# A decoder layer on one core: the order of the convolution's transfers on GpSimd, and the place of the rotary keys

## The chip, the core and the metric

The kernel runs on one NeuronCore of a Trainium2 chip. The core has five engines, each with its own queue, worked off in order: TensorE (PE in the profile; its weight loads are PEld), VectorE (DVE), ScalarE (ACT), GpSimd (POOL) and SyncE (SP). SyncE only issues transfers here. ScalarE and GpSimd issue a few as well; all transfers run on the core's DMA engines. An instruction waits in its engine's queue until the work it depends on has finished, and everything behind it in that queue waits too.

The metric is the device time of one execution in microseconds, the median of several runs. Before the change it is 1056.4 us over 3 runs (1056.02 to 1057.13).

## The reference

One layer over 256 tokens of width 2048, all in float32. Cut to what matters:

```python
h = _rmsnorm(x, pre_norm_g)
proj = h @ w_in       # split into q_a, c_kv, k_rope, z_mla, c_in, b_gate, c_gate, z_conv, g_mla, g_conv
q  = _rmsnorm(q_a, q_a_norm_g) @ w_q_b        # 16 heads of 128 (nope) + 64 (rope)
kv = _rmsnorm(c_kv, kv_a_norm_g) @ w_kv_b     # 16 heads of 128 (k_nope) + 128 (v)
q_rope, k_rope = _apply_rope(q_rope, cos, sin), _apply_rope(k_rope, cos, sin)
# per head: scores = q_nope . k_nope + q_rope . k_rope, causal softmax, times v
y_mla  = (attn * silu(z_mla)) @ w_o_mla
u      = c_gate * c_in
conv   = conv_w[0] * u[t-2] + conv_w[1] * u[t-1] + conv_w[2] * u[t]
y_conv = (b_gate * conv * silu(z_conv)) @ w_o_conv
merged = sigmoid(g_mla) * y_mla + sigmoid(g_conv) * y_conv
x + _rmsnorm(merged @ w_out, post_norm_g)
```

The rotary part of the keys, `k_rope`, is one vector of 64 numbers per token, shared by all heads. Rotation needs a cosine and a sine for each position and frequency.

## The kernel before

**Products in two parts.** Every weight arrives as float32 and is split into a high part (`whi`, a rounded copy made by ScalarE, L224) and a low part (`wlo`, the rest, made by VectorE, L225). Activations are split likewise. A product of two such pairs takes three matmuls. The weights form one list, `plan`, of units of 128 x 2048 floats (1 MB); `take` hands out a unit and runs ahead of it: three raw units are loaded by SyncE (`load_raw`, L144) and one is split in advance (`split_unit`). A raw buffer is loaded again when its splits are done; split buffers (5 of each part) are free again when TensorE has read them.

**The order of work.** The program is built by a scheduler that places instructions on each engine by its own cost estimates and what they depend on. An instruction wrapped in `tc.keep_in_program_order` keeps, against the others so wrapped on its engine, the order in which the program text issues it. All matmuls and transposes are wrapped (L86, L89), so TensorE's order is the text's.

**The start.** The first eight units (`u_qa`) hold the activations and the query projection side by side; `latent_products` (L423) makes `qa` from them, six matmuls for each 128 features, and then `ckv`. The first three of these units go to raw buffers, the next three (the list `early`) to memory that other tiles use later: the profile shows them as `cv_f<-xw_dram` and `at_f<-xw_dram`. GpSimd meanwhile makes the rotary tables (`tables`, L359): it loads the positions, reduces the angles, and after ScalarE's sine (L398, L399) copies the results with 32 small copies (L406) to `cos_t` and `sin_t`. Its queue also holds the inverse roots of the norms (L319): `r_ckv` stands behind these copies.

**The rotary keys.** The product `kr` gives the unrotated keys in `kr_f`, which is a part of `at_f`. `key_rope` (L490) scales them (`rows`, L350) and rotates them: `rp_a` is the tile times the cosine (L416), four pieces `rp_b` the swapped quarters times the sine (L419), their sum goes back to `at_f` (L420), and `split_act` makes the two parts of `kr`, the high one on ScalarE and the low one on VectorE. First to read `kr` are the scores of head 0 (`sc<-kr,qr`). `key_rope` is called in `turn_keys`, between the two halves of the first convolution product of head 0, right after the sign is put on `sin_t` (L409).

**The first group.** Heads go in groups of two. `group_a(0)` makes `qn` and `kn` for both heads, `group_b(0)` makes `qr` (with its own rope, L524) and `vv`. Their results leave PSUM through four banks tagged `mm`, in turn: qn0, qn1, kn0, kn1, then qr takes the bank of qn0, and the two vv those of qn1 and kn0. A bank is free when VectorE has added its two halves (`whole`, L347, the tile `f`).

**The heads.** For each of 16 heads the text runs the gate product z, the scores, four quarters of a convolution product (`channels`, tile `cv`), and in between transposes, values and the next group's products. In head 0 the scores come after `channels(0, 2)`.

**The convolution.** Every fourth head completes one of four inputs for a block of 512 channels. After heads 1 and 2 of each four, `taps` (L648) is started, first for the upper 128 tokens (t = 1), then for the lower ones (t = 0). It brings the inputs shifted by one and two tokens into `mv` tiles (L654, L657; a memset L656 for the tokens before the first), and the taps, one row of 512 weights repeated over all 128 partitions, into `cw` tiles (L661, two buffers). A step later VectorE multiplies and adds (L665), and the third `cw` is loaded. All these transfers are issued by GpSimd; before the change they are not wrapped.

**The end.** `tokens` makes the merged gates and branches (tiles `sq`), then the output product (`out`), the norm and the store.

Of the kernel before, what the change touches and what calls it, by code (L numbers as in the profile page):

```python
# [18 lines left out]
P = 128  # L19
# [61 lines left out]
def tile_layer(ctx: ExitStack, tc: tile.TileContext, xw, x, pos, pvec, post_g, wc, wz, wcv, wkr, wqk, wrv, cwr, wsq, out):  # L81
    nc = tc.nc
# [111 lines left out]
    def take(i):  # L194
        ahead(i)
        parts = splits.pop(i)

        def piece(j, n):
            o = j * n
            h, o = o // HALF, o % HALF  # L200
            return parts[h][0][:, o : o + n], parts[h][1][:, o : o + n]

        return piece

    def bank(name, tag="mm", bufs=4):
        return psum.tile([P, 512], F32, name=name, tag=tag, bufs=bufs)

    def product(ps, a, b, first, last):

        (ah, al), (bh, bl) = a, b  # L210
        matmul(ps, ah, bh, start=first, stop=False)
        matmul(ps, ah, bl, start=False, stop=False)
        matmul(ps, al, bh, start=False, stop=last)
# [9 lines left out]
    def split_act(hi, lo, src, keep=False):  # L223
        a = nc.scalar.activation(hi, src, AF.Copy)  # L224
        b = nc.vector.tensor_tensor(lo, src, hi.bitcast(F32), op=ALU.subtract)  # L225
        if keep:

            tc.keep_in_program_order(a)
            tc.keep_in_program_order(b)
# [57 lines left out]
    def temp(name, shape=(P, S), dt=F32, bufs=2, tag=None):  # L287

        tag, n = tag or name.rstrip("0123456789_"), shape[-1]
        if n % LINE == 0:  # L290
            return bp.tile(list(shape), dt, name=name, tag=tag, bufs=bufs)
        return bp.tile([P, -(-n // LINE) * LINE], dt, name=name, tag=tag, bufs=bufs)[:, :n]
# [56 lines left out]
    def rows(dst):  # L349
        nc.vector.tensor_tensor(dst, dst, r_x[:, :], op=ALU.mult)  # L350

    def project(u, name, both=x_both, **kw):
        w = take(u)
        ps = bank(name, **kw)
        halves([(ps, w(k, P), both[:, k, :], k == 0, k == KD - 1) for k in range(KD)])
        return ps
# [56 lines left out]
    def rope(src, dst):  # L413

        a, b = temp("rp_a", bufs=1), temp("rp_b", bufs=1)
        nc.vector.tensor_tensor(a[:, :], src, cos_t[:, :], op=ALU.mult)  # L416
        for q in range(4):
            i, o = slice(32 * q, 32 * q + 32), slice(32 * (q ^ 1), 32 * (q ^ 1) + 32)
            nc.vector.tensor_tensor(b[o, :], src[i, :], sin_t[i, :], op=ALU.mult)  # L419
        nc.vector.tensor_tensor(dst, a[:, :], b[:, :], op=ALU.add)  # L420
# [69 lines left out]
    def key_rope():  # L490
        rows(kr_f)
        rope(kr_f, kr_f)
        split_act(kr[:, 0, :], kr[:, 1, :], kr_f)


    def pair(name, shape, bufs=1):
        return [temp(f"{name}_{n}", shape, F32R, bufs, tag=f"{name}_{n}") for n in ("hi", "lo")]
# [3 lines left out]
    def narrow(name, w, j, src):  # L501
        ps = bank(name)
        halves([(ps, w(j * KR + k, P), src[:, k, :], k == 0, k == KR - 1) for k in range(KR)])
        f = temp("f")
        whole(f[:, :], ps)
        return f
# [13 lines left out]
    def group_b(g):  # L520
        qr, vv = temp("qr", (P, HG, S), F32R, 1), pair("vv", (P, NT, HG * DV))
        w = take(u_grp[g][1])
        f = narrow(f"qr{g}", w, 0, qa)
        rope(f[:, :], f[:, :])  # L524
        for j in range(HG):

            own, other = (slice(DR * i, DR * i + DR) for i in (j, 1 - j))
            split_act(qr[own, j, :], qr[other, j, :], f[own, :])
        for t in range(NT):
            ps = bank(f"vv{g}_{t}")  # L530
            for k in range(KR):
                c = [ckv[:, k, o + t * P : o + (t + 1) * P] for o in (0, S)]
                product(ps[:, :S], c, w(2 + k, HG * DV), k == 0, k == KR - 1)
            split_act(vv[0][:, t, :], vv[1][:, t, :], ps[:, :S])
        groups[g] += [qr, vv]
# [42 lines left out]
    def turn(h, p):  # L578

        tp = bank(f"tp{h}", tag="st", bufs=1)  # L580
        for b in range(3):
            transpose(tp[:, b * P : (b + 1) * P], p[:, b * P : (b + 1) * P], ident[:, :])
        pt = temp("pt", (P, 2, 3 * P), F32R, 1)
        split_act(pt[:, 0, :], pt[:, 1, :], tp[:, : 3 * P])
        return pt
# [15 lines left out]
    def silu(name, ps):  # L601
        f, s = temp("sl_f", bufs=1), temp(name)
        whole(f[:, :], ps)
        rows(f[:, :])
        nc.scalar.activation(s[:, :], f[:, :], AF.Sigmoid)
        nc.vector.tensor_tensor(s[:, :], f[:, :], s[:, :], op=ALU.mult)
        return s
# [8 lines left out]
    cv_t = cv_f[:, :, :].rearrange("p (j t k) s -> p j t (k s)", j=4, t=NT)  # L616
    cv_ps = {}

    def channels(h, i, between=None):

        if i == 0:
            cv_ps["now"] = [bank(f"cv{h}_{t}", tag="cv", bufs=2) for t in range(NT)]
        w = take(u_head[h][1 + i])
        for t in range(NT):
            if t and between:
                between()
            for k4 in range(4):
                k = 4 * i + k4
                a = [x_both[:, k, o + t * P : o + (t + 1) * P] for o in (0, S)]
                product(cv_ps["now"][t][:, :], a, w(k4, 512), k == 0, k == KD - 1)  # L630
        if i == 3:
            channels_done(*divmod(h, 4))

    def channels_done(j, n):
        for t in range(NT):
            ps, r = cv_ps["now"][t], r_col[:, t : t + 1]
            w, u = cv_w[:, t, :], cv_t[:, j, t, :]
            if n == 0:
                nc.scalar.activation(u, ps[:, :], AF.Copy, scale=r)
            elif n == 2:  # L640
                nc.scalar.activation(w, ps[:, :], AF.Sigmoid, scale=r)
            if n:
                dst = u if n == 1 else w
                nc.vector.scalar_tensor_tensor(dst, ps[:, :], r, dst, op0=ALU.mult, op1=ALU.mult)
            if n == 3:
                nc.vector.tensor_tensor(u, u, w, op=ALU.mult)

    def taps(j, t):  # L648

        u, parts = cv_t[:, j, t, :], []  # L650
        for d in (1, 2):
            m = temp(f"mv{d}", (P, 512), bufs=1, tag=f"mv{d}x")
            if t:
                nc.gpsimd.dma_start(out=m[:d, :], in_=cv_t[P - d :, j, 0, :])  # L654
            else:
                nc.gpsimd.memset(m[:d, :], 0.0)  # L656
            nc.gpsimd.dma_start(out=m[d:, :], in_=u[: P - d, :])  # L657
            parts.append(m[:, :])
        def tap(d):
            cw = temp("cw", (P, 512), bufs=2)  # L660
            nc.gpsimd.dma_start(out=cw[:, :], in_=cwr[2 - d : 3 - d, 512 * j : 512 * (j + 1)].to_broadcast([P, 512]))  # L661
            return cw

        def join(dst, a, b, op):
            tc.keep_in_program_order(nc.vector.tensor_tensor(dst, a, b, op=op))  # L665

        cws = [tap(d) for d in (1, 2)]
        yield
        for a, cw in zip(parts, cws):
            join(a, a, cw[:, :], ALU.mult)  # L670
        join(parts[0], parts[0], parts[1], ALU.add)
        cw = tap(0)
        yield
        join(u, u, cw[:, :], ALU.mult)
        join(u, u, parts[0], ALU.add)
        yield

    cv_w = bp.tile([P, NT, 512], F32, name="cv_w")
    for h in range(H):
        sz = silu("sz", project(u_head[h][0], f"z{h}"))  # L680
        if h == 0:
            latent_turn("qa", qa, "q_g", (("st", 1), ("o", 1)))
            def turn_keys():
                latent_turn("ckv", ckv, "kv_g", (("mm", 4), ("mm", 4)))
                next(table_parts)
                key_rope()
        else:
            if h == 1:
                values(0, pt, sz0)
            p = scores(h)  # L690
        channels(h, 0, None if h else turn_keys)
        if h == 0:
            group_a(0)
            group_b(0)
        channels(h, 1)
        if h > 0:
            pt = turn(h, p)
        if h % 4 > 1:
            next(tap)
        channels(h, 2)  # L700
        if h > 0:
            values(h, pt, sz)
            if h % 4 > 1:
                next(tap)
            values_next(h)
        else:
            p = scores(h)
        channels(h, 3)
        if h % 4 in (1, 2):

            tap = taps(h // 4, 2 - h % 4)
            next(tap)
        if h == 0:
            values_next(h)
            pt, sz0 = turn(h, p), sz
# [52 lines left out]
    for c in range(4):  # L768
# [12 lines left out]
        m = gates[0]  # L781
# [170 lines left out]
```

## Time and profile before

| what | before |
|---|---|
| median of 3 runs | 1056.4 us (1056.02 to 1057.13) |
| the profiled execution | 1056.16 us, its span 1054.4 us |
| granted TensorE clock | 0.998 |
| VectorE busy | 669.8 us (64%) |
| ScalarE busy | 563.2 us (53%) |
| GpSimd busy | 70.5 us (7%) |
| bytes moved | 212.17 MB, mean 201 GB/s |

The profile is of one execution. Times in it count from the start of the span in microseconds; a row of the order of time gives start, duration, engine, line, operation, output and inputs, and in square brackets how long the engine was idle before it and what ended that. "x4" after a form means that four neighbouring instructions were merged into the row. A line can be that of a helper, so all matmuls bear L86. Matmuls overlap: the next starts before the last has ended. In a table by stretches each engine has its busy time and the number of its instructions; the last three columns are the granted clock (1.00 is full), the mean busy share of the DMA engines and the bytes per second in GB.

### The profile page before, as it was taken

What the parts mean: (1) busy time and instruction counts of PE and PEld (TensorE: products, weight loads), DVE (VectorE), ACT (ScalarE), POOL (GpSimd) and SP (SyncE); (2) the same over time, 40 slices, a digit from 0 to 9 for tenths busy, and PEclk for the clock granted to TensorE, in tenths of its full rate; (3) what the DMA queues carried; (4) which work ended last, traced back from release to release, by engine and by line L of the source; (5) the groups of instructions that cost most, each with busy time, mean ns of one, the idle gap of its engine ahead of it and who ended that gap; (6) DMA issues with size and microseconds to landing.
All of it is one profiled execution on the core that took longest, in us unless ns stands there. A gap on an engine that the chain in (4) does not pass through costs nothing.

```text
span 1054.4 us, 13093 instructions
## 1 busy us (share of the span) xinstructions
PE 1044.4 (99%) x5030; PEld 879.5 (83%) x5030; DVE 669.8 (64%) x962; ACT 563.2 (53%) x778; POOL 70.5 (7%) x147
## 2 busy tenths in 40 slices
PE   9999999999999999999999999999999999999997
PEld 7888888888888888888888888888888888888885
DVE  7587677865787767777676765554554455445562
ACT  7777556566665566645656464434444434443450
POOL 7520010000010000100001000000000000000000
PEclk9999999999999999999999999999999999999999
DMA  8755466654675545755467455555555555558552
GB/s 324 313 193 190 160 220 200 229 200 150 220 229 200 200 166 205 235 194 200 156 217 246 172 198 176 184 200 184 188 190 196 200 190 187 182 200 307 195 176 80
DMA packets 33311, 212.17 MB, mean 201 GB/s; under 512 B 4256, under 2 KB 4960, under 8 KB 10848
## 3 DMA queue, kind: packets, MB, share of 16 engines
q1 hardware_dynamic: 29232, 197.54, 53.1%
q0 software_dynamic: 3584, 10.50, 3.6%
q10 hardware_dynamic: 432, 3.29, 0.8%
q8 instruction: 39, 0.64, 0.2%
q14 instruction: 24, 0.20, 0.1%
HBM read 205.05 MB, written 2.10 MB: 196 GB/s over the span
## 4 chain that ended last, share of the span: by engine, by line
PE 93%; POOL 2%; issue 1%; DVE 1%; DMA 1%; ACT 1%; SPq 0%; POOLq 0%; DVEq 0%; ACTq 0%
PE sq L86 33%; PE cv L86 33%; PE z L86 8%; PE out L86 7%; PE vv L86 2%; PE kn L86 2%; PE qn L86 2%; PE sc L86 1%; PE qa L86 1%; PE ckv L86 1%; DMA cv_f<-xw_dram 1%; PE qr L86 1%; PE o L86 1%; POOL cos_t L406 1%; POOL sin_t L406 1%
## 5 line engine op out<-in xcount | busy, mean ns | idle before, releaser
L225 DVE TENSOR_TENSOR wlo<-raw,whi 128x1024 fp32r<-128x1024 f32 (+1 forms) x370 | 440.8, 1199 | 308.9 <-ACT whi L224 279.4
L224 ACT ACTIVATE whi<-raw 128x1024 fp32r<-128x1024 f32 (+1 forms) x372 | 384.0, 1036 | 370.3 <-PE sq L86 187.5
L86 PE MATMUL cv<-whi,x_both 128*128 128x512 f32 x1024 | 325.5, 391 | 0.0
L86 PEld LDWEIGHTS cv<-whi,x_both 128*128 128x128 f32 x1024 | 192.3, 188 | 38.7
L86 PE MATMUL cv<-wlo,x_both 128*128 128x512 f32 x512 | 199.6, 390 | 0.0
L86 PE MATMUL sq<-whi,x_both 128*128 128x512 f32 x512 | 160.2, 391 | 0.0
L86 PEld LDWEIGHTS sq<-whi,x_both 128*128 128x128 f32 x512 | 96.1, 188 | 19.8
L86 PEld LDWEIGHTS cv<-wlo,x_both 128*128 128x128 f32 x512 | 96.2, 188 | 18.5
L86 PE MATMUL sq<-wlo,x_both 128*128 128x512 f32 x256 | 99.6, 389 | 0.0
L86 PE MATMUL sq<-whi,at_both 128*128 128x512 f32 x256 | 80.4, 391 | 0.0
L86 PE MATMUL sq<-whi,cv_both 128*128 128x512 f32 x256 | 79.4, 389 | 0.0
L86 PE MATMUL out<-whi,m_both 128*128 128x512 f32 x256 | 79.3, 390 | 0.0
L86 PE MATMUL z<-x_both,whi 128*128 128x512 f32 x256 | 60.8, 390 | 0.0
L86 PEld LDWEIGHTS sq<-whi,cv_both 128*128 128x128 f32 x256 | 48.1, 188 | 10.0
L86 PEld LDWEIGHTS sq<-whi,at_both 128*128 128x128 f32 x256 | 48.1, 188 | 9.9
L86 PEld LDWEIGHTS out<-whi,m_both 128*128 128x128 f32 x256 | 48.1, 188 | 9.9
L86 PEld LDWEIGHTS sq<-wlo,x_both 128*128 128x128 f32 x256 | 48.1, 188 | 9.8
L86 PEld LDWEIGHTS z<-x_both,whi 128*128 128x128 f32 x256 | 47.9, 188 | 9.9
L86 PE MATMUL sq<-wlo,at_both 128*128 128x512 f32 x128 | 49.8, 389 | 0.0
L86 PE MATMUL sq<-wlo,cv_both 128*128 128x512 f32 x128 | 49.8, 389 | 0.0
L86 PE MATMUL out<-wlo,m_both 128*128 128x512 f32 x128 | 49.8, 389 | 0.0
L86 PEld LDWEIGHTS z<-x_both,wlo 128*128 128x128 f32 x256 | 32.8, 191 | 1.2
(209 smaller groups left out, 1068.1 us busy)
## 6 DMA issues: line engine op xcount, KB each, us to landing
raw<-wsq_dram SPq DMA_DIRECT2D x80, 1024.0 KB, 4.7
raw<-wcv_dram SPq DMA_DIRECT2D x64, 1024.0 KB, 4.8
raw<-wz_dram SPq DMA_DIRECT2D x16, 1024.0 KB, 4.7
raw<-wqk_dram SPq DMA_DIRECT2D x8, 1024.0 KB, 5.8
cw<-cwr_dram POOLq DMA_DIRECT2D x24, 256.0 KB, 4.0
raw<-wrv_dram SPq DMA_DIRECT2D x8, 768.0 KB, 4.3
raw<-wc_dram SPq DMA_DIRECT2D x4, 1024.0 KB, 10.0
cv_f<-x_dram SPq DMA_DIRECT2D x1, 2048.0 KB, 9.4
```

The source lines that it names most:

```text
L86: return tc.keep_in_program_order(nc.tensor.matmul(*a, **kw))
L224: a = nc.scalar.activation(hi, src, AF.Copy)
L225: b = nc.vector.tensor_tensor(lo, src, hi.bitcast(F32), op=ALU.subtract)
L406: tc.keep_in_program_order(nc.gpsimd.tensor_copy(dst[to, SQ * q : SQ * (q + 1)], src[ti, :]))
```

## The change

The transfers and memsets of `taps` are now wrapped in `keep_in_program_order`, through a small function `bring`. And `key_rope()` is called no more in `turn_keys` but after `group_b(0)`.

```diff
     def taps(j, t):
 
         u, parts = cv_t[:, j, t, :], []
+
+        def bring(dst, src):
+
+            tc.keep_in_program_order(nc.gpsimd.dma_start(out=dst, in_=src))
+
         for d in (1, 2):
             m = temp(f"mv{d}", (P, 512), bufs=1, tag=f"mv{d}x")
             if t:
-                nc.gpsimd.dma_start(out=m[:d, :], in_=cv_t[P - d :, j, 0, :])
+                bring(m[:d, :], cv_t[P - d :, j, 0, :])
             else:
-                nc.gpsimd.memset(m[:d, :], 0.0)
-            nc.gpsimd.dma_start(out=m[d:, :], in_=u[: P - d, :])
+                tc.keep_in_program_order(nc.gpsimd.memset(m[:d, :], 0.0))
+            bring(m[d:, :], u[: P - d, :])
             parts.append(m[:, :])
         def tap(d):
             cw = temp("cw", (P, 512), bufs=2)
-            nc.gpsimd.dma_start(out=cw[:, :], in_=cwr[2 - d : 3 - d, 512 * j : 512 * (j + 1)].to_broadcast([P, 512]))
+            bring(cw[:, :], cwr[2 - d : 3 - d, 512 * j : 512 * (j + 1)].to_broadcast([P, 512]))
             return cw
...
             def turn_keys():
                 latent_turn("ckv", ckv, "kv_g", (("mm", 4), ("mm", 4)))
                 next(table_parts)
-                key_rope()
...
         if h == 0:
             group_a(0)
             group_b(0)
+            key_rope()
         channels(h, 1)
```

In the built program, GpSimd's queue before the change has two `cw` transfers right behind the four position loads at the start, ahead of the mask and the tables; after the change they stand behind the first four `mv` transfers, at the end of head 1. The later `cw` loads, which before stood as far ahead as their buffers allowed, now follow the `mv` transfers of their own block. On VectorE the first rope product of the keys (`rp_a`) moves from behind L350 of the keys, and the four `rp_b`, the sum and the low split of `kr` from among the group's operations, to the end of the group's operations: `rp_a` and `rp_b` behind the sum of the queries' rope, the sum behind the two low splits of `qr`, the low split of `kr` one weight split later. On ScalarE the high split of `kr` moves likewise. TensorE and SyncE have the same instructions in the same order.

## The prediction

> **What bounds the kernel now.** I read the first page, then the waits of TensorE, then the order of time on each engine from 4 to 17 us and from 59 to 90 us.
>
> ```profile
> PE 1044.4 (99%) x5030; PEld 879.5 (83%) x5030; DVE 669.8 (64%) x962; ACT 563.2 (53%) x778; POOL 70.5 (7%) x147
> PE 93%; POOL 2%; issue 1%; DVE 1%; DMA 1%; ACT 1%; SPq 0%; POOLq 0%; DVEq 0%; ACTq 0%
> ```
>
> TensorE is busy for 99% of the span and makes 93% of the chain that ended last. What VectorE, ScalarE or GpSimd lose or gain therefore counts only where TensorE stands still. Its waits say where that is:
>
> ```profile
> PE qa L86 <- ACT whi L224: 0.9, 1, 0.9
> PE qr L86 <- DVE f L347: 0.2, 1, 0.2
> ```
>
> These are two single waits, and both lie where the change reaches: one in the first query products, while the early loads run, and one in the first group's products. Busy time hides part of such a loss, because a product that waits is drawn longer, so I take each loss from the spacing of starts. The first, TensorE in order of time:
>
> ```profile
> 12.43 1.13 PE L86 MATMUL qa<-whi,x_both 128*128 128x512 f32 x4
> 13.40 0.62 PE L86 MATMUL qa<-wlo,x_both 128*128 128x512 f32 x2
> 14.94 1.19 PE L86 MATMUL qa<-whi,x_both 128*128 128x512 f32 x4 [0.92 <-ACT whi L224]
> 15.97 0.62 PE L86 MATMUL qa<-wlo,x_both 128*128 128x512 f32 x2
> 16.43 1.07 PE L86 MATMUL qa<-whi,x_both 128*128 128x512 f32 x4
> 17.35 0.62 PE L86 MATMUL qa<-wlo,x_both 128*128 128x512 f32 x2
> 17.80 0.39 PE L86 MATMUL qa<-whi,x_both 128*128 128x512 f32 x1
> ```
>
> A step of six products takes 17.80 - 16.43 = 1.37. Two steps from 12.43 would end at 15.17; the next one begins at 16.43. **The early loss is 1.26 us.** The second place, with the same shapes of the next group behind it, from the chain of waits:
>
> ```profile
> 71.48 1.09 PE L86 MATMUL kn<-ckv,whi 128*128 128x512 f32 x4
> 72.42 0.63 PE L86 MATMUL kn<-ckv,wlo 128*128 128x256 f32 x4
> 73.20 1.19 PE L86 MATMUL qr<-qa,whi 128*128 128x512 f32 x4 [0.15 <-DVE f L347]
> 74.24 0.63 PE L86 MATMUL qr<-qa,wlo 128*128 128x256 f32 x4
> 75.00 0.38 PE L86 MATMUL vv<-whi,ckv 128*128 128x256 f32 x1
> 75.23 0.28 PE L86 MATMUL vv<-wlo,ckv 128*128 128x256 f32 x1
> ```
>
> ```profile
> 125.71 1.40 PE qr L86 x8
> 127.11 2.88 PE vv L86 x24
> ```
>
> Undisturbed, such a block of eight (kn has the shapes of qr) takes 1.40 and one vv product 2.88 / 24 = 0.12. So qr was due at 72.88, vv at 74.28 and its second product at 74.40; it began at 75.23. **The group's loss is 0.83 us.** Together 2.09 us: the most that removing these two waits can return.
>
> **Part 1: two cw transfers leave the start.** The tap weights `cw` depend on nothing, and before the change the scheduler put the first two at the head of GpSimd's queue; now they stand behind the four `mv` transfers at the end of head 1. At the start they run while the weights of the first products arrive. GpSimd's issue, its queue from 4 to 13 us, and the DMA share there and a little later:
>
> ```profile
> 3.99 1.10 POOL L661 DMA_DIRECT2D cw<-cwr_dram  x2
> ```
>
> ```profile
> q0 software_dynamic: 287, 0.56, 25.1%
> ```
>
> ```profile
> 4.00:13.00 9.00, 9.00 (x40) 7.45 (x39) 7.04 (x13) 5.75 (x11) 5.57 (x13) 1.00 1.02 339
> 18.00:22.00 4.00, 4.00 (x19) 3.31 (x18) 4.00 (x8) 4.00 (x10) 3.32 (x9) 1.00 1.02 427
> 69.20:87.60 18.40, 18.11 (x98) 15.43 (x97) 18.10 (x34) 11.37 (x21) 0.00 (x0) 1.00 0.52 185
> ```
>
> The DMA engines are full in 4 to 13 us (share 1.02), and GpSimd's queue has 25.1% of them: 0.56 MB, nearly all of it the two `cw` (128 x 512 floats each, 0.52 MB together). What TensorE waits for at 14.94 is ScalarE, and ScalarE waits for the fourth load:
>
> ```profile
> 13.86 0.51 ACT L299 ACTIVATE x_both<-cv_f,pv 128x256 fp32r<-128x256 f32 x1 [1.54 <-DMA cv_f<-xw_dram]
> 14.28 0.61 ACT L224 ACTIVATE whi<-cv_f 128x512 fp32r<-128x512 f32 x1
> ```
>
> Without the two transfers this load lands earlier by 0.52 MB at the 427 GB/s that the weights reach alone at 18 to 22 us, 1.23 us, or by up to 25.1% of 9 us = 2.26 us. TensorE was due at 12.43 + 1.37 = 13.80 instead of 14.94, so a landing 1.14 earlier is enough, and both prices exceed it. After that ScalarE needs 0.51 + 0.61 for a step against 1.37 on TensorE, so it is not late next. The later loads are issued as VectorE frees buffers and move along with it. Bounds: 0 (the freed time is not given to this load) to 1.26. With the engines full I take **1.26**.
>
> The 1.10 us of issue also leaves GpSimd's table work; that work is done long before it is used, so I count nothing. The two transfers now go out behind the `mv` ones. Their new cover, in GpSimd's queue and on VectorE, and the landing of all 24:
>
> ```profile
> 137.71 1.07 POOL L657 DMA_DIRECT2D mv<-cv_f  x2 [1.38 <-DVE cv_f L644]
> ```
>
> ```profile
> 155.62 1.29 DVE L665 TENSOR_TENSOR mv<-mv,cw 128x512 f32<-128x512 f32 x2
> ```
>
> ```profile
> DMA to landing us min/median/max: 3.6/4.0/8.8
> ```
>
> Issued from 137.71 + 1.07 = 138.8 to 139.9, they land by 148.7 at the slowest of the 24, and VectorE multiplies by them at 155.62. Cost 0, with 6.9 us of cover; if it were gone, VectorE's weight splits would queue behind that multiplication, late by as much. The other convolution blocks get the same order. The swaps among `mv` and memset instructions move nothing past a deadline.
>
> **Part 2: the rotary keys go behind the group.** Before, `rp_a`, four `rp_b`, the sum into `at_f` and the split into `kr` stand between VectorE's work on the first group:
>
> ```profile
> L419 DVE TENSOR_TENSOR rp_b<-at_f,sin_t x4: 414/416/420, 69.8 to 71.1; 32x256 f32<-32x256 f32 x4
> L420 DVE TENSOR_TENSOR at_f<-rp_a,rp_b x1: 418/418/418, 73.1 to 73.1; 128x256 f32<-128x256 f32 x1
> ```
>
> ```profile
> L86 PE MATMUL sc<-kr,qr x3: 282/282/335, 89.1 to 89.7; 128*128 128x256 f32 x3
> L224 ACT ACTIVATE kr<-at_f x1: 418/418/418, 73.5 to 73.5; 128x256 fp32r<-128x256 f32 x1
> L225 DVE TENSOR_TENSOR kr<-at_f,kr x1: 421/421/421, 75.2 to 75.2; 128x256 fp32r<-128x256 f32 x1
> ```
>
> The sum `f` that frees the bank for qr stands behind the four `rp_b`, 1.67 us; qr is late by 73.20 - 72.88 = 0.32. The `f` for vv stands behind 1.67 + 0.42; vv is late by 0.72. Both waits go: **0.83 gained**, nothing if another input of these products is late, which the waits do not name.
>
> What is late next is the keys. In the built order their last piece now stands behind the group's rope, the `qr` splits and three weight splits. The last of these, and `vv_lo` on the way, on VectorE:
>
> ```profile
> 86.37 1.23 DVE L225 TENSOR_TENSOR wlo<-raw,whi 128x1024 fp32r<-128x1024 f32 x1
> ```
>
> ```profile
> 78.33 0.42 DVE L225 TENSOR_TENSOR vv_lo<-vv,vv_hi 128x256 fp32r<-128x256 f32 x1
> ```
>
> From 69.20 to 87.60 VectorE is busy for 18.10 of 18.40 us (the third stretch above), so the same work in another order ends at 86.37 + 1.23 = 87.60, with `kr` last. To that comes `rp_a`, which was done earlier and now falls into this run, 0.4 (the size of `at_f`'s row): 88.0. And VectorE, 1.67 + 0.42 + 0.42 = 2.5 earlier, now meets `vv_lo` at 75.8, while TensorE ends the first vv block at 74.28 + 1.44 = 75.7 and ScalarE needs some 0.4 for its high part (the size of its `kr` row): 0.4 of waiting. So `kr` is ready between 88.0 and 88.4. TensorE needs it at 89.1 - 0.83 = 88.3. **Cost 0 to 0.2; I take 0.2**, a new wait in the scores of head 0. The 13 us of cover that the keys had (75.2 to 89.1) is gone: each further us of delay on VectorE now costs a us.
>
> Such a delay has a source in the trace. GpSimd's 32 table copies stand ahead of `r_ckv`, with which the run on VectorE begins:
>
> ```profile
> L406 POOL COPY cos_t<-ta_m x16: 228/232/1215, 44.1 to 58.4; 32x64 f32<-32x64 f32 x16
> ```
>
> ```profile
> 47.28 2.60 DVE L225 TENSOR_TENSOR wlo<-raw,whi 128x1024 fp32r<-128x1024 f32 x2
> 47.49 1.13 POOL L406 COPY cos_t<-ta_m 32x64 f32<-32x64 f32 x1
> ```
>
> One form takes 0.23 or up to 1.2 us, and the 1.13 us copy lies under a VectorE split that reads two tiles: 0.9 us for each meeting. The Trainium skill (SBUF — State Buffer, "SBUF: two separate sides") gives the reason: GpSimd shares a port pair with VectorE as an exclusive lock, and a VectorE operation with two SBUF inputs holds off a GpSimd operation that reads SBUF. By that rule, with which this row agrees, an edit that shifts the two engines against each other changes the number of meetings. Here both shift by nearly the same, so I put nothing into the sum for it.
>
> **Sum.** 1.26 + 0.83 - 0.2 = 1.9 us. The profiled execution took 1056.16 (its span 1054.4 and 1.76 around it), so 1054.3 in its terms. It lies 0.24 below the median of 1056.4; on the median the forecast is **1054.5**.
>
> **The rivals.**
> 1. *The early gain does not reach the end*: the fourth load lands as before, or TensorE starts sooner but the table chain (and with it `kr`) does not move, and the scores wait 88.4 - (88.3 - 1.26) = 1.4. Left: 0.83 - 0.2 = 0.6, or 2.09 - 1.4 = 0.7: 1055.7. For it: the table chain hangs on a long row of loads and squares. Against: full DMA engines ahead of each of them.
> 2. *More*: the transfers cost 2.26 us of DMA time, VectorE gets further ahead than TensorE and the keys are in time. Then 2.09 are gained: 1054.3, or a little less with what else the early loads cost. For it: only 339 GB/s with the two, 427 without.
> 3. *Keys late, slower*: VectorE meets the first scores with more meetings on GpSimd ahead of it. From `kr` at 88.3 + 2.09 = 90.4, two meetings (1.8) past 88.4, the kernel is no faster; four or five (3.6 to 4.5) give 1054.5 + 4.0 = 1058.5. For it: the cover of 13 us is gone. Against: the same copies and splits stand in that stretch.
>
> **How the numbers follow.** The forecast 0.56, rival 1 0.14, rival 2 0.16, rival 3 0.14. A measurement of this kernel can tell about 0.2%, 2.1 us, from no change, and the forecast lies just inside; the three runs span 1.1 us. So I give 0.21 of the forecast's chance and 0.15 of rival 2's to faster, 0.10 of rival 3's to slower, and the rest to no change: 0.36, 0.54, 0.10. The forecast's own range is 1053.9 to 1055.2 (2.09 and the scatter below; 1.4 above); with rival 1 and the near part of rival 3 it is 1053.5 to 1056.8.
>
> **What would show it.** Right: no `cw` before 100 us, TensorE's third step in the quoted stretch at about 13.8 with no wait, qr and vv 1.40 apart behind kn, `kr` split some 0.5 us or less around the scores of head 0, and a wait of TensorE there of at most 0.3. Wrong: the wait of qa stands at 0.9; or the scores of head 0 wait for 1 us or more; or TensorE waits somewhere past 140 us.

## The result and the profile after

| | before | after |
|---|---|---|
| median of 12 runs each | 1056.62 us (1056.02 to 1058.50) | 1054.51 us (1054.20 to 1055.15) |
| after / before | | 0.9978, 95% interval 0.9969 to 0.9987 |
| the profiled execution | 1056.16 us, span 1054.4 us | 1054.46 us, span 1052.5 us |
| granted TensorE clock | 0.998 | 0.999 |

The change is worth 2.1 us, and the forecast was 1054.5. The interval lies below 1, so the gain is real, but it is small: 0.2%, about the size that the prediction called the least that can be told from no change. One execution of run 3 below took 2251.16 us, twice the usual, and is no part of the ratio there; the row of run 3 gives the median of all 11, 1057.17, and the other ten have 1056.98.

The page of after, the busy line and the chain that ended last:

```profile
PE 1043.5 (99%) x5030; PEld 879.1 (84%) x5030; DVE 669.8 (64%) x962; ACT 562.9 (53%) x778; POOL 72.2 (7%) x147
PE 97%; DVE 1%; issue 1%; ACT 0%; POOL 0%; POOLq 0%; DVEq 0%; ACTq 0%
```

TensorE now makes 97% of the chain instead of 93%, with the same work on every engine. Its waits, apart from one ahead of the first product that both kernels have:

```profile
PE sc L86 <- DVE kr L225: 0.2, 1, 0.2
```

Both waits of before (`qa`, `qr`) are gone, and one stands in their place. **The start**, TensorE and ScalarE in order of time:

```profile
12.19 1.07 PE L86 MATMUL qa<-whi,x_both 128*128 128x512 f32 x4
13.09 0.61 PE L86 MATMUL qa<-wlo,x_both 128*128 128x512 f32 x2
13.54 1.07 PE L86 MATMUL qa<-whi,x_both 128*128 128x512 f32 x4
14.45 0.61 PE L86 MATMUL qa<-wlo,x_both 128*128 128x512 f32 x2
14.90 1.07 PE L86 MATMUL qa<-whi,x_both 128*128 128x512 f32 x4
12.04 0.51 ACT L299 ACTIVATE x_both<-cv_f,pv 128x256 fp32r<-128x256 f32 x1 [0.86 <-DMA cv_f<-xw_dram]
```

The steps stand 1.36 apart with no wait. The fourth load reaches ScalarE at 12.04 instead of 13.86, and the eighth step of `qa` begins at 14.90 instead of 16.43: 1.53 us earlier. That the DMA engines deliver more shows in the stretches from 4 to 13 us (the last three columns are the granted clock, the DMA share and GB/s). First before, then after:

```profile
9.00:11.00 2.00, 2.00 (x10) 1.65 (x9) 1.42 (x3) 0.65 (x2) 1.51 (x3) 1.00 1.01 245
11.00:13.00 2.00, 2.00 (x11) 1.52 (x10) 1.16 (x2) 1.04 (x2) 1.68 (x5) 1.00 0.99 334
```

```profile
4.00:13.00 9.00, 9.00 (x41) 7.35 (x40) 7.36 (x14) 6.29 (x14) 4.10 (x10) 1.00 1.02 376
9.00:11.00 2.00, 2.00 (x9) 1.42 (x8) 1.96 (x5) 2.00 (x5) 1.17 (x2) 1.00 1.03 424
11.00:13.00 2.00, 2.00 (x10) 1.64 (x9) 1.40 (x3) 1.14 (x4) 1.75 (x4) 1.00 1.02 427
```

The engines are as busy in both, but before they moved 245 and 334 GB/s from 9 to 13 us, after 424 and 427.

**The group**, TensorE:

```profile
69.95 1.09 PE L86 MATMUL kn<-ckv,whi 128*128 128x512 f32 x4
71.35 1.09 PE L86 MATMUL qr<-qa,whi 128*128 128x512 f32 x4
72.76 0.28 PE L86 MATMUL vv<-whi,ckv 128*128 128x256 f32 x1
72.88 0.28 PE L86 MATMUL vv<-wlo,ckv 128*128 128x256 f32 x1
```

kn, qr and vv begin 1.40 apart and the second vv product 0.12 behind the first: the 0.83 us of the group are back.

**The scores of head 0.** TensorE before, then TensorE and VectorE after:

```profile
88.99 0.22 PE L86 MATMUL sc<-kn,qn_lo 128*128 128x128 f32 x1
89.05 0.34 PE L86 MATMUL sc<-kr,qr 128*128 128x256 f32 x1
```

```profile
86.66 0.22 PE L86 MATMUL sc<-kn,qn_lo 128*128 128x128 f32 x1
87.11 0.38 PE L86 MATMUL sc<-kr,qr 128*128 128x256 f32 x1 [0.23 <-DVE kr L225]
80.37 0.42 DVE L420 TENSOR_TENSOR f<-rp_a,rp_b 128x256 f32<-128x256 f32 x1
80.82 0.42 DVE L416 TENSOR_TENSOR rp_a<-at_f,cos_t 128x256 f32<-128x256 f32 x1
81.26 1.71 DVE L419 TENSOR_TENSOR rp_b<-at_f,sin_t 32x256 f32<-32x256 f32 x4
86.63 0.42 DVE L225 TENSOR_TENSOR kr<-at_f,kr 128x256 fp32r<-128x256 f32 x1
```

Undisturbed, the product on `kr` follows 0.06 behind; now 0.45. The wait's own row says 0.23, the spacing says that 0.39 us were lost. The product began 0.06 behind the end of `kr` at 87.05.

**The sum over the pair of profiles.** The first product of `qn` and the gate product of head 1, behind the scores, before and then after:

```profile
67.30 1.07 PE L86 MATMUL qn<-qa,whi 128*128 128x512 f32 x4
101.12 1.17 PE L86 MATMUL z<-x_both,whi 128*128 128x512 f32 x4
```

```profile
65.77 1.07 PE L86 MATMUL qn<-qa,whi 128*128 128x512 f32 x4
99.23 0.94 PE L86 MATMUL z<-x_both,whi 128*128 128x512 f32 x3
```

`qn` starts 1.53 earlier: all that the eighth step of `qa` gained, passed on whole over 50 us. From `qn` to the gate product it took 101.12 - 67.30 = 33.82, now 33.46: another 0.36. The group's 0.83 less the scores' 0.39 would be 0.44; the remaining 0.08 is in the spacing of the other blocks up to there. Together 1.89, and the spans differ by 1.9: nothing is won or lost behind the first 100 us. There the transfers stand where the change put them, at GpSimd, without a wait anywhere on TensorE:

```profile
135.82 1.61 POOL L654 DMA_DIRECT2D mv<-cv_f  x3 [1.93 <-DVE cv_f L644]
137.43 1.12 POOL L654 DMA_DIRECT2D cw<-cwr_dram  x2
```

### The profile page after: what moved, and what is told of

It is laid out like the page before. It is cut to its first block, busy times and chain, and to the rows that moved or that the text cites. A ratio compares the mean times of both kernels' runs of the same rounds, so it can differ in the third digit from the quotient of the medians.

```text
span 1052.5 us, 13082 instructions
## 1 busy us (share of the span) xinstructions
PE 1043.5 (99%) x5030; PEld 879.1 (84%) x5030; DVE 669.8 (64%) x962; ACT 562.9 (53%) x778; POOL 72.2 (7%) x147
## 4 chain that ended last, share of the span: by engine, by line
PE 97%; DVE 1%; issue 1%; ACT 0%; POOL 0%; POOLq 0%; DVEq 0%; ACTq 0%
PE sq L86 33%; PE cv L86 32%; PE z L86 8%; PE out L86 7%; PE kn L86 2%; PE qn L86 2%; PE qa L86 2%; PE ckv L86 2%; PE vv L86 2%; PE sc L86 1%; PE qr L86 1%; PE o L86 1%; PE tp L89 0%; PE idle L86 0%; PE kr L86 0%
## 5 line engine op out<-in xcount | busy, mean ns | idle before, releaser
L654 POOL DMA_DIRECT2D mv<-cv_f x24 | 12.9, 540 | 323.0 <-issue 159.7
```

The costliest lines, as they stand in the source:

```text
L654: tc.keep_in_program_order(nc.gpsimd.dma_start(out=dst, in_=src))
```

## The experiments

Two clocks are read in each run. **Eighth step** is the start of the eighth step of `qa` on TensorE (16.43 before, 14.90 after): what the start costs. **Keys** is the time from the first `qn` to the gate product of head 1 (33.82 and 33.46): what the place of the keys costs. The expectations give the second one to the next row of the gate product, 0.24 us later, so their 33.7 is 33.46 here and their 33.25 is 33.0. All runs of a kernel are compared with runs of the kernel before on the same chip (30 or 33 of them, median 1056.8 or 1056.9). An interval reaches about 1 us to each side, so what the place of the keys costs or gains, some 0.4 us, can be read only from the traces.

| run | what | median us | ratio to before, 95% | eighth step | keys |
|---|---|---|---|---|---|
| 1 | order of the transfers only | 1054.98 | 0.9982, 0.9973 to 0.9990 | 15.13 | 33.74 |
| 2 | place of the keys only | 1057.07 | 0.9999, 0.9990 to 1.0008 | 18.07 | 33.47 |
| 3 | after, two unread taps loads at the start | 1057.17 | 1.0001, 0.9992 to 1.0010 | 16.91 | 33.46 |
| 4 | after, cosine product of the keys early | 1054.25 | 0.9976, 0.9967 to 0.9985 | 15.25 | 33.00 |
| 5 | after once more | 1055.01 | 0.9982, 0.9973 to 0.9990 | 15.20 | 33.45 |
| 6 | after, all of the keys early | 1055.83 | 0.9986, 0.9977 to 0.9995 | 15.40 | 34.44 |
| 7 | after, two loads of 128 x 8 at the start | 1056.81 | 0.9999, 0.9990 to 1.0008 | 17.18 | 33.48 |
| 8 | after, two taps loads at 58 us | 1055.15 | 0.9983, 0.9974 to 0.9992 | 15.10 | 33.46 |
| 9 | after, two loads of 128 different rows | 1056.63 | 0.9997, 0.9988 to 1.0006 | 16.17 | 33.46 |
| 10 | after, two taps loads by SyncE | 1057.68 | 1.0006, 0.9997 to 1.0015 | 16.89 | 33.44 |
| 11 | after, two loads of one row | 1055.07 | 0.9983, 0.9974 to 0.9992 | 15.53 | 33.47 |
| 12 | run 4 once more | 1054.35 | 0.9975, 0.9965 to 0.9985 | 15.15 | 33.04 |

### Which part of the change gives what: runs 1, 2 and 3

Run 1 calls `key_rope` where it was and keeps the new order on GpSimd:

```diff
             group_b(0)
-            key_rope()
...
                 next(table_parts)
+                key_rope()
```

> Only the transfers keep their order; the keys stay ahead of the group. Theory (two separate places on TensorE): the early gain alone, 1.3 to 1.5 us off the kernel before (ratio 0.9986 to 0.9988); the wait of qa gone, the wait of qr on f (L347) back with its 0.83 us, no wait in the scores of head 0. Rival (the early gain only lives on because the keys no longer hold VectorE): TensorE starts sooner but waits the same time more at qr, and the kernel is as before within 0.4 us.

Measured: 1054.98. In the group, and at the scores:

```profile
70.17 1.09 PE L86 MATMUL kn<-ckv,whi 128*128 128x512 f32 x4
71.81 1.19 PE L86 MATMUL qr<-qa,whi 128*128 128x512 f32 x4
87.60 0.22 PE L86 MATMUL sc<-kn,qn_lo 128*128 128x128 f32 x1
87.66 0.34 PE L86 MATMUL sc<-kr,qr 128*128 128x256 f32 x1
```

qr was due at 71.57 and is 0.24 late (before 0.32), and the second vv product, at 73.84, is 0.75 late (before 0.83); the scores do not wait. So the group's loss belongs to the place of the keys and the scores' wait is what moving them costs. The gain at the start comes without the keys' move: 1.9 us against the kernel before, more than the 1.3 to 1.5 expected. The changed kernel in run 5 has the same median, 1055.01, so the medians do not show the gain from the keys' place; the traces do (33.74 here, 33.45 there).

Run 2 is the other half: the kernel before with `key_rope` behind `group_b(0)`.

```diff
                 next(table_parts)
-                key_rope()
...
             group_b(0)
+            key_rope()
```

> Only the keys move; two cw transfers stand at the head of GpSimd's queue again. Theory: qr and vv run without a wait (0.83 us gained), the scores of head 0 wait some 0.5 us for kr, so 0.3 to 0.4 us off the kernel before; the wait of qa stands at 0.9. Rival (the order of the later transfers or another effect makes the gain): 1 us or more.

Measured: 1057.07, the same as before within the interval, where 0.3 to 0.4 us less were expected, though the keys' clock stands at 33.47, 0.35 better. In the profiled execution the start took that back and more. TensorE waits for 2.7 us in `qa`, where 0.9 was expected. TensorE and ScalarE there:

```profile
16.58 1.20 PE L86 MATMUL qa<-whi,x_both 128*128 128x512 f32 x4 [2.23 <-ACT whi L224]
15.50 0.51 ACT L299 ACTIVATE x_both<-cv_f,pv 128x256 fp32r<-128x256 f32 x1 [3.00 <-DMA cv_f<-xw_dram]
```

The same load that came at 13.86 in the profile of before came at 15.50 here, with nothing changed ahead of it. The loss at the start varies from one execution to the next, and the profile of before that the forecast was read from shows a mild one.

Run 3 puts two loads of the taps, which nobody reads, back to the head of GpSimd's queue in the changed kernel:

```diff
+        for d in range(2):
+            cw = temp("cw", (P, 512), bufs=2)
+            tc.keep_in_program_order(
+                nc.gpsimd.dma_start(out=cw[:, :512], in_=cwr[d % 2 : d % 2 + 1, :512].to_broadcast([P, 512]))
+            )
         y, n1, n2, r = (temp(f"ta_{n}", (P, SQ), bufs=1) for n in "ymnr")
```

> The changed kernel with two loads of tap weights added at the head of GpSimd's queue, 0.52 MB in all, read by nobody; all later transfers keep the changed order. Theory (bytes among the early loads cost TensorE's step): the wait of qa is back, and the whole early gain is lost, 1.3 to 1.5 us above the changed kernel. Rival (the early gain came from the later order, or from a first load that landed earlier by chance): within 0.4 us of the changed kernel.

Measured: 1057.17; the eighth step at 16.91. Two loads at the start are enough to lose what the change had won, and more than the 1.3 to 1.5 us expected: it is 2.0 to 2.2 us above run 1 on the same chip. With before and run 2 the eighth step stands at 16.43, 18.07 and 16.91, mean 17.14; in the seven profiles with no added load at the start (after, runs 1, 4, 5, 6, 8, 12) at 14.90 to 15.40, mean 15.16. **The early gain is 2.0 us on average over these profiles**, where the one profile of before showed 1.26. With the loads there are only three of them, and they lie 1.6 us apart. The medians give somewhat less: 2.1 (result), 1.9 (run 1) and 1.8 us (run 5) in all, less what the keys' clock gains, leave 1.5 to 1.9 for the start.

### Does it repeat: run 5

The changed kernel unchanged.

> The changed kernel once more, on the chip of the three runs beside it. If the keys' place costs a fixed amount (theory): from the start of the first query-nope product qn to the first gate product behind the scores of head 0 it takes 33.7 us again, with about 0.45 us lost at the scores on kr. If the early products vary by themselves without the two tap loads (rival: the early gain of the first pair of profiles was chance), the eighth step of qa starts anywhere from 14.9 to 17; by the theory it starts between 14.9 and 15.3. Time 1054.5.

Measured: 1055.01, 0.5 above the forecast time and 1.8 below the kernel before on the same chip; eighth step 15.20, keys 33.45 and the scores at 86.95 and 87.41, again 0.46 apart. In the first pair 0.47 us of the 1.53 lay in the first step (4.99 to 6.49 after, 4.99 to 6.96 before); here that step is nearly as long as before, 1.90, and the eighth is still early. The place of the gain varies, the gain does not go.

### Where the keys cost least: runs 4, 12 and 6

Run 4 leaves the keys behind the group but makes their scaling and cosine product in `turn_keys`, before the group, when VectorE is not full:

```diff
+    def key_cos():
+        rows(kr_f)
+        nc.vector.tensor_tensor(kr_g, kr_f, cos_t[:, :], op=ALU.mult)
+
     def key_rope():
-        rows(kr_f)
-        rope(kr_f, kr_f)
+        rope(kr_f, kr_f, kr_g)
...
                 next(table_parts)
+                key_cos()
```

> The changed kernel, but the scaling of the keys and their product with the cosine are done where they were before (written to a free part of at_f), and only the sine products, the sum and the split go behind the group. Theory (VectorE's unbroken run sets when kr is ready, each operation in it a us for a us): kr is ready 0.43 us sooner and the wait in the scores of head 0 falls from about 0.46 to 0 to 0.1, so 0.3 to 0.45 us off the changed kernel. Rival (kr waits for ScalarE or for a weight split that TensorE releases): no change.

> The changed kernel with only the cosine product of the keys made early, once more beside the three others. Theory: TensorE has no wait in the scores of head 0, 33.25 us from the first qn to the gate product behind the scores, against 33.7 in the changed kernel; 1054.1 to 1054.6. Rival (the scores' wait gone in the first profile was chance): 33.7 and a wait of 0.2 or more on kr.

Measured: 1054.25 and 1054.35, keys 33.00 and 33.04. TensorE in run 4:

```profile
87.01 0.22 PE L86 MATMUL sc<-kn,qn_lo 128*128 128x128 f32 x1
87.07 0.34 PE L86 MATMUL sc<-kr,qr 128*128 128x256 f32 x1
```

The scores' wait is gone and the group is still undisturbed. One operation of 0.42 us fewer on VectorE between 65 and 87 us is worth 0.42 to 0.46 us: there VectorE has no slack. The medians stand 0.2 to 0.8 below those of the changed kernel, which the intervals do not separate; that it is better rests on the trace of the two runs.

Run 6 makes all of the keys early, ahead of the transposes:

```diff
+            next(table_parts)
+            key_rope()
             latent_turn("qa", qa, "q_g"
...
             group_b(0)
-            key_rope()
```

> The changed kernel with the sign of the sine and the keys called ahead of the transposes of qa, so that on VectorE the four rp_b come between the two halves of ckv and the rest ahead of the sums of qn. Theory (VectorE is full from 65 to 87 us, so 2.5 us of keys ahead of the group's sums come late somewhere in the group): no wait in the scores, but 0.6 to 1.0 lost in kn, qr and vv; qn to the gate product 33.9 to 34.3, time 1054.7 to 1055.2. Rival (early is early enough: the idle 1.15 us of VectorE ahead of sz takes them up): 33.25 and 1054.1, as with the cosine product made early.

Measured: 1055.83, keys 34.44. VectorE and TensorE in it:

```profile
66.38 1.71 DVE L419 TENSOR_TENSOR rp_b<-at_f,sin_t 32x256 f32<-32x256 f32 x4
68.12 0.88 DVE L455 SCALAR_TENSOR_TENSOR ckv<-lt_ckv,pv,ckv 128x256 fp32r<-128x256 f32 x2
69.84 0.87 DVE L455 SCALAR_TENSOR_TENSOR ckv<-lt_ckv,pv,ckv 128x256 fp32r<-128x256 f32 x2
70.38 1.18 PE L86 MATMUL kn<-ckv,whi 128*128 128x512 f32 x4 [1.18 <-DVE ckv L455]
```

The four `rp_b` stand ahead of `ckv`, and kn waits for its second half. The theory had the right sign, but 1.4 us are lost against run 12 where it gave 0.6 to 1.0, and the time is above its 1054.7 to 1055.2; the place was kn alone. Earlier is worse than before the change (33.82), and the idle time of VectorE ahead of `sz` did not take the keys up.

### What the two loads cost at the start: runs 7 to 11

The forecast priced them by bytes. Run 7 keeps two loads at the head of the queue and takes the bytes away:

```diff
-                nc.gpsimd.dma_start(out=cw[:, :512], in_=cwr[d % 2 : d % 2 + 1, :512].to_broadcast([P, 512]))
+                nc.gpsimd.dma_start(out=cw[:, :8], in_=cwr[d % 2 : d % 2 + 1, :8].to_broadcast([P, 8]))
```

(against run 3)

> The changed kernel with two unread loads at the head of GpSimd's queue, of 128 x 8 floats each in place of 128 x 512: the same two issues and the same 128 rows each, 8 KB in place of 0.52 MB. If the bytes among the early loads cost the time (theory): as the changed kernel, 1054.5, the eighth step of qa at 14.9 to 15.3. If the issue on GpSimd (about 1.1 us) or the number of pieces of the transfer costs it (rival): 1056.5 to 1057.2, the eighth step at 16.4 to 18.1.

Measured: 1056.81, eighth step 17.18. **The theory that only bytes cost falls**: within the intervals 8 KB cost as much as 0.52 MB. The rival has two readings, the issue on GpSimd or the pieces.

Run 8 asks whether such a load costs wherever it stands: run 3's loads, issued behind `r_ckv`.

```diff
+            for d in range(2):
+                cw = temp("cw", (P, 512), bufs=2)
+                tc.keep_in_program_order(
+                    nc.gpsimd.dma_start(out=cw[:, :512], in_=cwr[d % 2 : d % 2 + 1, :512].to_broadcast([P, 512]))
+                )
             group_a(0)
             group_b(0)
```

> The changed kernel with two unread loads of 128 x 512 floats on GpSimd's queue behind r_ckv, at about 58 us, where the DMA engines are busy for 0.39 of the time. If such a load only costs where it pushes back a load that TensorE is waiting for (theory): 1054.5, no new wait of TensorE. If the transfers cost wherever they run, by their traffic into SBUF (rival): 1056 to 1057, as at the head.

Measured: 1055.15 with 15.10 and 33.46, as the changed kernel. At 58 us TensorE has no load to wait for, and the same loads cost nothing.

Runs 9, 10 and 11 vary what is left. Run 9 reads 128 different rows of x in place of one row 128 times; run 10 lets SyncE issue the loads of the taps, ahead of the fourth load; run 11 loads one row of 512 floats each to one partition.

```diff
+            tc.keep_in_program_order(nc.gpsimd.dma_start(out=cw[:, :], in_=x[:, d, :512]))
```

```diff
+        if i == u_qa[2]:
+            for d in range(2):
+                cw = temp("cw", (P, 512), bufs=2)
+                nc.sync.dma_start(out=cw[:, :], in_=cwr[d : d + 1, :512].to_broadcast([P, 512]))
```

```diff
+            tc.keep_in_program_order(nc.gpsimd.dma_start(out=cw[:1, :], in_=cwr[d : d + 1, :512]))
```

> The changed kernel with two unread loads of 128 x 512 floats at the head of GpSimd's queue that read 128 different rows of x instead of one row of the taps 128 times: 0.52 MB, as many pieces, the same queue. Theory (the many pieces that read one and the same row hold the DMA engines): only the bytes count, 1.23 us against about 1 us by which the fourth load is early in the changed kernel, so the eighth step of qa starts at 15.2 to 15.9 and the time is 1054.5 to 1055.2; from 9 to 11 us the DMA engines move 400 GB/s or more. Rival (each piece on GpSimd's queue holds an engine, whatever it reads): the eighth step at 16.4 to 18.1, 1056.3 to 1057.2, from 9 to 11 us 350 GB/s or less.

> The changed kernel with two unread loads of the taps, repeated over the partitions as in the kernel, issued by SyncE ahead of the fourth load of the query weights. Theory (the pieces that read one row hold the engines): as at the head of GpSimd's queue, the eighth step of qa at 16.4 to 18.1, 1056.3 to 1057.2. Rival (GpSimd's queue is what costs): the bytes alone, the eighth step at 15.2 to 15.9, 1054.5 to 1055.2.

> The changed kernel with two unread loads of one row of 512 floats each (4 KB together) at the head of GpSimd's queue: two issues there, and two pieces in place of 256. Theory (the pieces cost, by one row or by the queue): no cost, the eighth step of qa at 14.9 to 15.4, 1054.5 to 1055. Rival (the issue on GpSimd itself, which also holds up the mask and the tables): 16.4 to 18.1, 1056.3 to 1057.2.

Measured: 1056.63, 1057.68 and 1055.07. Run 11 has the same two issues on GpSimd and takes as long as the changed kernel: the issue is not the cost. Run 10 does not use GpSimd's queue for these loads, and loses as much: that queue is not needed for the cost. (There the fourth load is issued 1.06 us later, at 4.62 against 3.56 in after, and stands behind the two in its own queue, so the run does not price one queue against the other.) Run 9 reads no row twice, and loses too: one row read many times is not needed for a cost. What those that lose share, down to run 7 with 32 bytes in each, is 256 rows to be written, 128 in each load. That the rows are the cause is not shown by this: run 9 also moves 0.52 MB, run 7 also reads one row many times, and no run loads a few bytes each from 128 different rows. GpSimd's queue from 4 to 13 us (packets, MB, share of the 16 engines) in runs 7, 11 and 9 and after, in this order:

```profile
q0 software_dynamic: 192, 0.04, 13.9%
```

```profile
q0 software_dynamic: 192, 0.04, 3.3%
```

```profile
q0 software_dynamic: 287, 0.56, 17.5%
```

```profile
q0 software_dynamic: 128, 0.03, 3.5%
```

Runs 7 and 11 have the same packets and, to 0.01 MB, the same bytes, but run 7 four times the time: 10.6% of 9 us on 16 engines, 15.3 us, over 254 more rows is 0.06 us of an engine for a row of 32 bytes. In run 9 it is 14.0% over the 3.5% of after, 20.2 us over 256 rows: 0.08 for a row of 2 KB. At 427 GB/s, 26.7 for an engine, 2 KB take 0.077. So on average a row of 32 bytes held an engine nearly as long as one of 2 KB, and the 25.1% that the prediction quotes for the loads of before, less 3.5%, make 0.12 for each row: there one row is read many times.

The average hides what the single packets in the traces show. In run 7 the two loads are 32 packets of 256 bytes, eight rows each: twelve took 18 or 19 ns, the other twenty 278 to 1345. So a row of 32 bytes needs little in itself, and most of that time is a hold-up. In run 9 the loads are 128 packets of two rows, 4 KB, and most took 159 ns, as the shortest did; together they held the engines for 22.1 us, 1.4 us for each of 16. That is near the 1.23 us of the price by bytes, and the eighth step of run 9 is 1.0 later than the mean without loads. The same 128 packets that read one row many times add up to more: 33.6 us in before, 27.0 in run 2, 25.3 in run 3. This fits two costs, the bytes and a hold-up where one row is read many times, at least as well as a cost by rows; it was not tested further.

The Trainium skill (DMA: Bandwidth & Descriptors, "Measured (HBM→SBUF, 128 partitions, SWDGE, issued from GpSimd)") gives 0.68 us for a load of 4 KB over 128 partitions and puts it down to a smallest number of packets. By that figure two of them would take 1.4 us, an estimate; run 7 against run 5 lost 1.8, which is of that order. The reason given is not borne out here: run 11 has as many packets as run 7 by the profile's count (192) and lost nothing.

How many bytes the engines then move is another matter. The stretch from 9 to 11 us in runs 9, 10 and 7:

```profile
9.00:11.00 2.00, 2.00 (x10) 1.65 (x9) 1.96 (x4) 1.66 (x4) 0.70 (x2) 1.00 1.03 399
```

```profile
9.00:11.00 2.00, 2.00 (x10) 1.65 (x10) 2.00 (x5) 1.82 (x4) 1.32 (x4) 1.00 1.06 205
```

```profile
9.00:11.00 2.00, 1.57 (x7) 1.05 (x6) 1.74 (x4) 1.71 (x4) 0.54 (x2) 1.00 0.90 164
```

Where one row of the taps is read many times, on either queue, the engines fall to 164 and 205 GB/s while they look busy (before 245, runs 2 and 3 347 and 354); with different rows they stay at 399, and without such loads no profile shows less than 415. In run 7 the rows are also short, so few bytes would move in any case. The rate does not rank the losses: before had 245 GB/s and the mildest loss of the kernels that read one row many times, run 2 had 347 and the largest. The theory of run 9 was right about this stretch, but for 1 GB/s, and wrong about the time; its eighth step, 16.17, lies between the two forecasts. Its profiled execution took 1055.97, below its median, so part of what its other executions lose is not seen. It stays open how much of the cost at the start is the bytes, the number of rows, or the row they share.

## Why the prediction was right, and where it was off

- *What bounds*: right. Removing the two named waits carried the gain, and nothing behind 100 us moved.
- *Part 1, the early loss, 1.26*: the mechanism was right and the size too small. The third of the quoted steps came at 13.54 without a wait (forecast 13.8). In the pair of profiles the start gave 1.53, over all profiles 2.0, by the medians 1.5 to 1.9, because the loss was read from one execution and varies: 16.43, 17.18, 16.91 and 18.07 were seen for the eighth step in the kernels with two taps loads on GpSimd. The gain lies between its two prices, 1.23 by bytes and 2.26 by the share of the DMA engines. Bytes alone are not the cause, as run 7 shows; run 9, where the price by bytes nearly holds in the trace, shows that they may be part of it.
- *The bounds of that term* ended at 1.26, what TensorE was seen to lose. That cut off the true value: the bound held for that one execution only.
- *The new cover of the transfers, 0*: right, and TensorE waits nowhere past 90 us.
- *Part 2, the group, 0.83*: right; kn, qr and vv stand 1.40 apart, and run 1 brings back 0.75 of the loss.
- *The keys, 0.2 of 0 to 0.2*: the place was right, the size too small: 0.38 to 0.41 in every run with all of the keys behind the group. Due at 86.72 in the profile of after, which is 88.25 in before's time (forecast 88.3), `kr` was ready at 87.05 or 88.58 (forecast 88.0 to 88.4). VectorE was idle for 0.61 of the 19.4 us up to there instead of 0.30, and busy for 18.77 instead of 18.10 + 0.42 = 18.52. Most operations of 0.42 start 0.34 behind the one before them, some 0.44 or 0.45 (80.37, 80.82, 81.26 above); that the new order has more such neighbours is read from the rows and was not tested by itself.
- *The sum, 1.9*: 1.53 + 0.36 in the pair of profiles, where 1.26 and 0.83 - 0.2 = 0.63 stood. The errors of the two parts, 0.27 each, cancelled; that the total is better than its parts is luck.
- *Rival 1* (the early gain does not reach the end): no; `qn` starts 1.53 earlier. *Rival 2* (more): right in that the start gives more than 1.26, wrong in that the keys come in time; with the keys in time, run 4 is what it describes, 1054.25 against its 1054.3. *Rival 3* (keys late by several us): no. The 0.4 us repeat in every run, so the meetings of GpSimd and VectorE did not vary it. That each us on VectorE now costs a us is what run 4 shows, for the 0.42 us of one operation; in run 6 it is kn that waits, for `ckv`.

## What to carry to other kernels

A load that depends on nothing was moved here by the scheduler to the head of its queue, where it competed with the first loads that the program does wait for; give such a load a place in the order close to its use. Do not price it by its bytes alone: two loads of 4 KB, one short row read for 128 partitions, cost 1.8 us at the start, and two of 256 KB cost nothing at 58 us, where no one waited for a load. And take a wait in the first 20 us from several executions before it is put into a sum: here it varied by more than the whole gain of the other part.

## What the hardware showed that was not expected

- Two loads of together 0.52 MB and two of together 8 KB cost the same at the start, within the intervals (1057.17 and 1056.81 against 1055.01); both read one row for 128 partitions. Packets of 256 bytes took 18 to 1345 ns there.
- With many reads of one row the DMA engines moved 164 to 354 GB/s from 9 to 11 us, at a busy share of 0.90 to 1.06, whichever queue issued them; with different rows it was 399, without such loads 415 or more. A busy DMA share does not say that bytes move.
- The kernels with 256 rows at the start scatter: 1055.83 to 1058.92 in run 7, 1056.33 to 1059.28 in run 10. Without them: 1054.73 to 1055.61 in run 5, and with two rows alone 1054.64 to 1055.55 in run 11. Most of the scatter between executions goes with the two loads.
